# Block with expert retrieval on one core: scores picked by one-hot products, 896 output columns by a weight matrix built on chip

## The chip, the core and the metric

The kernel runs on one core of a Trainium2 chip. The core has TensorE (PE, matrix products), VectorE (DVE), ScalarE (ACT), GpSimd (POOL) and SyncE (SP), which run side by side, and 16 DMA engines that move data between memory (HBM) and the on-chip SBUF. PE writes its results into PSUM. The metric is device time in microseconds of one execution; lower is better.

## The reference

One decoder block on 256 tokens of 2,048 columns in float32: attention and retention with their projections, then a layer of retrieved experts, then a norm. The change touches the experts alone:

```python
expert_idx = ...                     # 8 heads x 16 chosen of 16,384 experts for each token
gates = jax.nn.softmax(best_s, axis=-1)
u = expert_down[ib]                  # chosen rows, 2,048 columns
act = jax.nn.gelu(jnp.einsum('td,thkd->thk', xb, u), approximate=False)
vv = expert_up[ib]
return jnp.einsum('thk,thkd->td', gb * act, vv)
```

Each token thus has 128 chosen experts. An expert's number is 128 i + j, with i and j from 0 to 127.

## The kernel before

Projections, attention, retention and the query's scores take the time up to about 892 us. Then `gemm1` runs: 32 tiles of 512 experts, in which TensorE multiplies all tokens with the first 1,408 columns of `expert_down`. Weights come as `raw` on SyncE's queue, ScalarE rounds them to `whi` (L107), VectorE subtracts to `wlo` (L108), and PE takes three products of the parts (L154 to L156); 384 of the 1,408 columns are multiplied as plain fp32 (L161), which the trace shows as two instructions for each product. Each finished tile is scaled on ScalarE (L467) and written to `a_dram`, a 256 x 16,384 table of scores (L468).

The remaining 640 columns are fetched for the chosen experts only. This goes on as background work beside `gemm1`: `later` queues steps with a cost, and `drain` lets so many through after each piece of a tile (`BG_RATE`, `BG_NATIVE`); top 16, candidates and ranks come first, then `indices` (L586), then 256 steps `dot`. Step n holds 128 tokens on partitions and one of their 128 choices: GpSimd fetches one row per token (L605, eight buffers), and VectorE multiplies by `hg` and sums along the columns in one instruction (L613).

After the last tile comes the tail. `score` (L640) picks one 4-byte number per token from `a_dram` on GpSimd, 256 times, 14 ahead; `fetch` (L583) brings 128 whole rows of `expert_up`, 1 MB, into one of eight buffers. Both are issued in one line on GpSimd. For eight choices at a time VectorE adds the score and the dot (L680), ScalarE takes Gelu (L681), VectorE multiplies by the gate (L682); then each fetched row is multiplied by its weight and added to `ys` in PSUM (L687, L689). `finish` adds the result to `h` (L659), takes squares (L661), multiplies by `fin` (L662), scales by the root and stores (L673). A scheduler that places each instruction on its engine sets the order; the program's text gives it priorities.

## Time and profile before

| what | us |
|---|---|
| median of three runs | 2114.41 (2112.65 to 2115.06) |
| the profiled execution | 2116.2 |
| its span in the trace | 2114.4 |
| PE busy | 1387.9 (66%) |
| DVE busy | 1556.2 (74%) |
| ACT busy | 614.7 (29%) |
| POOL busy | 918.4 (43%) |
| bytes moved by DMA | 630.24 MB, mean 298 GB/s |

The shares are means over stages with different limits, so a stage's own rows matter more: in the page's 40 slices PE shows nines up to two thirds of the span and zeros after, the DMA engines nines from about 970 us on, and the granted clock of PE falls from nine to five tenths where PE's work ends. A busy time counts an engine's instructions, not what it waits for; the granted clock says which of PE's two levels, 1.2 or 2.4 GHz, held.

### The profile page before, as it was taken

The page shows a single profiled execution, that of the slowest core. Times are in us where ns is not written, and L with a number is a line of the kernel's source. Part 1 is how long each engine was busy: PE and PEld are TensorE (multiplying, and loading weights), DVE is VectorE, ACT ScalarE, POOL GpSimd, SP SyncE. Part 2 cuts the span into 40 slices and gives each one's busy share as a digit, 9 for nine tenths or more (in the row PEclk, how much of TensorE's full clock was granted, in tenths as well). Part 3 has the DMA queues.
Part 4 walks back from the last instruction along what each step waited for, and adds up shares of the span by engine and source line. Part 5 has one row for each costly group of instructions (what it writes and reads, how often), then busy time and mean ns, then how long its engine had stood idle before and what let it go on. Part 6 is the DMA issues. An engine that isn't in the chain of part 4 may idle for free.

```text
span 2114.4 us, 18649 instructions
## 1 busy us (share of the span) xinstructions
PE 1387.9 (66%) x5864; PEld 1076.1 (51%) x5864; DVE 1556.2 (74%) x2037; ACT 614.7 (29%) x780; POOL 918.4 (43%) x802
## 2 busy tenths in 40 slices
...
GB/s 313 183 151 176 175 144 197 221 197 187 193 189 192 191 231 162 176 194 325 406 406 391 391 408 408 396 353 271 395 397 395 399 399 384 410 400 407 399 400 307
DMA packets 114516, 630.24 MB, mean 298 GB/s; under 512 B 21872, under 2 KB 22512, under 8 KB 54000
## 3 DMA queue, kind: packets, MB, share of 16 engines
...
## 4 chain that ended last, share of the span: by engine, by line
PE 47%; DMA 20%; issue 17%; POOL 8%; DVE 8%; POOLq 0%; ACT 0%; ACTq 0%; DVEq 0%; SPq 0%
PE acc L139 13%; PE acc L138 13%; PE acc L140 13%; DMA v<-in_down_g_dram,ix 11%; DMA v<-in_up_dram,ix 6%; DVE ys L689 4%; POOL v L583 4%; POOL wsel L640 3%; PE acc L161 2%; DMA wsel<-a_dram,ix 2%; DVE wlo L108 1%; PE acc L155 1%; PE acc L156 1%; PE acc L154 1%; POOL v L605 1%
## 5 line engine op out<-in xcount | busy, mean ns | idle before, releaser
L108 DVE TENSOR_TENSOR wlo<-raw,whi 128x1024 fp32r<-128x1024 f32 (+1 forms) x426 | 526.1, 1236 | 332.9 <-ACT whi L107 332.5
L107 ACT CAST whi<-raw 128x1024 fp32r<-128x1024 f32 (+1 forms) x426 | 443.8, 1048 | 667.7 <-PE acc L140 367.5
L689 DVE SCALAR_TENSOR_TENSOR ys<-v,wsel,ys 128x2048 f32<-128x2048 f32 x254 | 598.3, 2355 | 30.8 <-DMA v<-in_up_dram,ix 23.3
L605 POOL DMA_INDIRECT v<-in_down_g_dram,ix x256 | 347.5, 1357 | 353.0 <-ACT whi L107 273.0
L640 POOL DMA_INDIRECT wsel<-a_dram,ix x256 | 259.1, 1012 | 96.4 <-issue 93.0
L583 POOL DMA_INDIRECT v<-in_up_dram,ix x256 | 260.9, 1019 | 80.7 <-issue 58.7
L613 DVE SCALAR_TENSOR_TENSOR djunk<-v,rs_r,hg 128x640 bf16<-128x640 f32 x256 | 219.2, 880 | 99.6 <-DMA v<-in_down_g_dram,ix 99.0
L139 PE MATMUL acc<-wlo,xth 128*128 128x512 f32 x736 | 291.9, 397 | 0.0
L140 PE MATMUL acc<-whi,xtl 128*128 128x512 f32 x736 | 288.2, 392 | 0.0
L138 PE MATMUL acc<-whi,xth 128*128 128x512 f32 x736 | 266.7, 394 | 9.1 <-ACT whi L107 9.1
L155 PE MATMUL acc<-wlo,hth 128*128 128x512 f32 x512 | 203.8, 398 | 13.1 <-DVE wlo L108 12.9
L156 PE MATMUL acc<-whi,htl 128*128 128x512 f32 x512 | 200.1, 391 | 0.0
L154 PE MATMUL acc<-whi,hth 128*128 128x512 f32 x512 | 191.4, 411 | 2.2 <-ACT whi L107 2.2
L681 ACT ACTIVATE wsel<-wsel 128x8 f32<-128x8 f32 x32 | 6.6, 208 | 595.9 <-DVE wsel L680 533.7
L161 PE MATMUL acc<-raw,htf 128*128 128x512 f32 x384 | 169.9, 592 | 0.0
L138 PEld LDWEIGHTS acc<-whi,xth 128*128 128x128 f32 x736 | 138.7, 189 | 38.3 <-ACT whi L107 9.5
L139 PEld LDWEIGHTS acc<-wlo,xth 128*128 128x128 f32 x736 | 138.8, 189 | 29.7 <-DVE wlo L108 1.0
L140 PEld LDWEIGHTS acc<-whi,xtl 128*128 128x128 f32 x736 | 138.8, 189 | 28.1 <-issue 0.2
L433 POOL TENSOR_TENSOR sg<-sg 128x512 f32<-128x512 f32 x8 | 14.1, 1790 | 291.8 <-DVE sg L432 291.8
L155 PEld LDWEIGHTS acc<-wlo,hth 128*128 128x128 f32 x512 | 96.1, 188 | 42.9 <-DVE wlo L108 22.2
L154 PEld LDWEIGHTS acc<-whi,hth 128*128 128x128 f32 x512 | 96.1, 188 | 33.5 <-issue 12.2
L161 PEld LDWEIGHTS acc<-raw,htf 128*128 128x128 f32 x384 | 72.7, 189 | 79.1 <-issue 76.6
...
## 6 DMA issues: line engine op xcount, KB each, us to landing
raw<-in_w_in_dram SPq DMA_DIRECT2D x91, 1024.0 KB, 4.8
raw<-in_down_dram SPq DMA_DIRECT2D x64, 1024.0 KB, 8.9
...
raw<-in_w_rb_dram SPq DMA_DIRECT2D x16, 1024.0 KB, 4.8
raw<-in_w_out_dram SPq DMA_DIRECT2D x16, 1024.0 KB, 4.8
raw<-in_w_q_dram SPq DMA_DIRECT2D x16, 1024.0 KB, 4.8
...
raw<-in_w_ab_dram SPq DMA_DIRECT2D x8, 1024.0 KB, 4.9
```

The source lines that it names most:

```text
L107: nc.scalar.copy(hi[:, k:k + step], src)
L108: nc.vector.tensor_sub(lo[:, k:k + step], src, hi[:, k:k + step].bitcast(F32))
L138: nc.tensor.matmul(ps[b], lhsT=xh, rhs=wh, start=(c == 0), stop=False)
L139: nc.tensor.matmul(ps[b], lhsT=xh, rhs=wl, start=False, stop=False)
L140: nc.tensor.matmul(ps[b], lhsT=xl, rhs=wh, start=False, stop=(c == last))
L154: nc.tensor.matmul(ps[b], lhsT=xh, rhs=wh, start=(c == 0), stop=False)
L155: nc.tensor.matmul(ps[b], lhsT=xh, rhs=wl, start=False, stop=False)
L161: nc.tensor.matmul(ps[b], lhsT=xf[:, k, b * P:(b + 1) * P], rhs=nat[:, k], start=False, stop=(k == CN - 1))
L583: return nc.gpsimd.indirect_dma_start(v, None, up, IndirectOffsetOnAxis(ap=ix[:, 0, b, k:k + 1], axis=0), bounds_check=NE - 1)
L605: nc.gpsimd.indirect_dma_start(u[:, :GC], None, down_g, IndirectOffsetOnAxis(ap=ix[:, 0, b, k:k + 1], axis=0), bounds_check=NE - 1)
L640: return nc.gpsimd.indirect_dma_start(wsel[:, b, k:k + 1], None, a_flat, IndirectOffsetOnAxis(ap=ix[:, 1, b, k:k + 1], axis=0), bounds_che ...
L689: nc.vector.scalar_tensor_tensor(ys, v, w[:, kk:kk + 1], ys, op0=OP.mult, op1=OP.add)
```

## The change

Output columns 0 to 895 (`DC`) no longer come from fetched rows. For them a matrix W of weights is built in SBUF, one slice of 128 x 128 for each j: W[i, j, t] is the weight of expert 128 i + j for token t, zero where the expert wasn't chosen. Then the output is a dense product of W with all 16,384 rows of `expert_up` in those columns: 64 chunks of 917,504 B on SyncE's queue, two buffers `ud`, eight fp32 products of 448 columns each (L765). The other 1,152 columns (`VC`) are fetched as before, in five buffers (L617 to L620), and added on VectorE (L710, L712).

The build takes four tokens at a time, in two halves of 128 tokens (`W0`, `W1`):

- `extract` (L653): SyncE reads the four tokens' scores back from `a_dram` as `at`, i on partitions, j along (L657). For eight tokens at a time VectorE compares the chosen i with a row of numbers (L661), and ScalarE casts the result into `hot`, three buffers (L664). PE transposes each token's `hot` (L669), ScalarE copies it to `hotT` (L671), and PE multiplies with `at` (L674): row k then holds all 128 j of the choice k. VectorE compares with the chosen j, multiplies and sums (L678), which picks the score.
- `weigh` (L681): for eight tokens, add the dot (L684), Gelu on ScalarE (L685), times gate (L686).
- `place` (L688), up to three groups later: VectorE puts each weight into its column j (L695), PE multiplies `hot` with that (L699), ScalarE copies the result into W with a stride of 512 B (L700).

After each half PE transposes the weights (L749), VectorE copies them to `wsel` (L750), and from then on `add_row` may run for that half of the tokens. The text has 32 `add_row` steps in the second half of the build and 224 beside the dense stage. `indices` now transposes the chosen i, j and gates to choices on partitions (`selT`), and the dots are transposed after each 128. `DOT`, a dot's cost in the background queue, goes from 0.85 to 1.15; the dots have eight buffers of their own. Picks of scores on GpSimd, and the line they stood in, are gone. Buffers that `gemm1` used are closed ahead of the build, and the build's ahead of the dense stage, so that W and `ud` can take their place.

```diff
-DOT = 0.85
-VR = 8
-GRP = 8
-LEAD = 14
+DOT = 1.15
+UR = 8
+VR = 5
+DC = 896
+HC = DC // 2
+VC = D - DC
+JU = 2
...
-    a_flat = a_dram.rearrange("t (e o) -> (t e) o", o=1)
+    a_keys = a_dram.rearrange("t (i j) -> i t j", j=P)
...
-    ix = peer.tile([P, 2, NB, P], U32, name="ix")
-    vtiles = {}
-    vp = {}
-
-    def fetch(n):
-        v = vp["pool"].tile([P, D], F32, name="v", bufs=VR)
-        b, k = divmod(n, P)
-        vtiles[n] = v
-        return nc.gpsimd.indirect_dma_start(v, None, up, IndirectOffsetOnAxis(ap=ix[:, 0, b, k:k + 1], axis=0),
-                                            bounds_check=NE - 1)
+    ix = peer.tile([P, NB, P], U32, name="ix")
+    utiles, vtiles = {}, {}
+    pl = {}
 
     def indices():
+        ef = rp.tile([P, NB, P], F32, name="ef")
+        nc.vector.scalar_tensor_tensor(ef, sel[:, 0], 128.0, sel[:, 1], op0=OP.mult, op1=OP.add)
+        nc.vector.tensor_copy(ix, ef)
+        for k in range(3):
+            pt = ms.tile([P, T], F32, name="ms")
+            for b in range(NB):
+                nc.tensor.transpose(pt[:, b * P:(b + 1) * P], sel[:, k, b], ident)
+            nc.scalar.copy(selT[:, k], pt)
+        nc.vector.tensor_copy(selB, selT[:, 0])
+        nc.vector.tensor_copy(irow, iota[:, :, None].to_broadcast([P, P, 2]))
         rt.close()
         msk.close()
-        tmp2 = pool("tmp2")
-        ef = tmp2.tile([P, 2, NB, P], F32, name="ef")
-        nc.vector.scalar_tensor_tensor(ef[:, 0], sel[:, 0], 128.0, sel[:, 1], op0=OP.mult, op1=OP.add)
-        for b in range(NB):
-            nc.vector.tensor_scalar_add(ef[:, 1, b], ef[:, 0, b], rows[:, b:b + 1])
-        nc.vector.tensor_copy(ix, ef)
-        vp["pool"] = pool("v")
-        vp["ps"] = pool("ysum", space=PSUM)
-        for n in range(VR):
+        pl["v"] = pool("v")
+        pl["ys"] = pool("ysum", space=PSUM)
+        pl["ex_stack"], pl["pa_stack"] = ExitStack(), ExitStack()
+        pl["ex"] = pool("ex", stack=pl["ex_stack"])
+        pa = pl["pa"] = pool("pa", stack=pl["pa_stack"])
+        hg = pl["hg"] = pa.tile([P, NB, GC], F32, name="hg")
+        for b in range(NB):
+            nc.scalar.dma_start(hg[:, b], bass.AP(tensor=frow.tensor, offset=frow.offset + G0, ap=[[0, P], [1, GC]]))
+            nc.vector.tensor_mul(hg[:, b], h[:, b, G0:], hg[:, b])
+        for n in range(UR):
             fetch_u(n)
 
-    utiles = {}
-
     def fetch_u(n):
-        u = vp["pool"].tile([P, D], F32, name="v", bufs=VR)
+        u = pl["pa"].tile([P, GC], F32, name="u", bufs=UR)
         b, k = divmod(n, P)
-        nc.gpsimd.indirect_dma_start(u[:, :GC], None, down_g, IndirectOffsetOnAxis(ap=ix[:, 0, b, k:k + 1], axis=0),
+        nc.gpsimd.indirect_dma_start(u, None, down_g, IndirectOffsetOnAxis(ap=ix[:, b, k:k + 1], axis=0),
                                      bounds_check=NE - 1)
         utiles[n] = u
+
+    def fetch_v(n):
+        v = pl["v"].tile([P, VC], F32, name="v", bufs=VR)
+        b, k = divmod(n, P)
+        nc.gpsimd.indirect_dma_start(v, None, up_g, IndirectOffsetOnAxis(ap=ix[:, b, k:k + 1], axis=0),
+                                     bounds_check=NE - 1)
+        vtiles[n] = v
 
     def dot(n):
         u = utiles.pop(n)
         b, k = divmod(n, P)
-        junk = peer.tile([P, GC], BF16, name="djunk", bufs=2)
-        nc.vector.scalar_tensor_tensor(junk, u[:, :GC], rstd2[:, b:b + 1], hg[:, b], op0=OP.mult, op1=OP.mult,
+        junk = pl["pa"].tile([P, GC], BF16, name="djunk", bufs=2)
+        nc.vector.scalar_tensor_tensor(junk, u, rstd2[:, b:b + 1], pl["hg"][:, b], op0=OP.mult, op1=OP.mult,
                                        accum_out=sdot[:, b, k:k + 1])
-        if n + VR < NB * P:
-            fetch_u(n + VR)
-        else:
-            fetch(n + VR - NB * P)
-
-    later(4.0, indices)
+        if n + UR < NB * P:
+            fetch_u(n + UR)
+        if k == P - 1:
+            pt = acc.tile([P, 512], F32, name="acc")
+            nc.tensor.transpose(pt[:, :P], sdot[:, b], ident)
+            nc.scalar.copy(selT[:, 3, b * P:(b + 1) * P], pt[:, :P])
+
+    later(6.0, indices)
     for n in range(NB * P):
         later(DOT, dot, n)
 
...
     for t in range(NT):
         gemm1(t)
-    drain(1e9)
-
-    wsel = peer.tile([P, NB, P], F32, name="wsel")
+
     part3 = cst.tile([P, NB, 4], F32, name="part3")
     o_rows = out.rearrange("(b p) d -> p b d", p=P)
     total = NB * P
-
-    def score(n):
+    for st in reversed(right):
+        st.close()
+    wp = [ExitStack() for _ in range(NB)]
+    hots = {}
+    W = [pool("w0", stack=wp[0], side="right").tile([P, P, P], F32, name="W0")]
+
+    def extract(b, g):
+        ex = pl["ex"]
+        t0 = b * P + 4 * g
+        at = ex.tile([P, 4, P], F32, name="at", bufs=2)
+        nc.sync.dma_start(at, a_keys[:, t0:t0 + 4, :])
+        if g % 2 == 0:
+            hb = ex.tile([P, 4, P, 2], BF16, name="hb")
+            ids = selB[:, t0:t0 + 8].rearrange("p (a t) -> p a t", t=2)
+            nc.vector.tensor_tensor(hb, irow[:, None].to_broadcast([P, 4, P, 2]),
+                                    ids[:, :, None, :].to_broadcast([P, 4, P, 2]), op=OP.is_equal)
+            hot8 = ex.tile([P, 8, P], F32, name="hot", bufs=3)
+            nc.scalar.copy(hot8.rearrange("p (a t) i -> p a i t", t=2), hb)
+            hots[t0], hots[t0 + 4] = hot8[:, :4], hot8[:, 4:]
+        hot = hots[t0]
+        pt = acc.tile([P, 512], F32, name="acc")
+        for q in range(4):
+            nc.tensor.transpose(pt[:, q * P:(q + 1) * P], hot[:, q], ident)
+        hotT = ex.tile([P, 4, P], F32, name="hotT", bufs=2)
+        nc.scalar.copy(hotT, pt.rearrange("p (q k) -> p q k", q=4))
+        pr = acc.tile([P, 512], F32, name="acc")
+        for q in range(4):
+            nc.tensor.matmul(pr[:, q * P:(q + 1) * P], lhsT=hotT[:, q], rhs=at[:, q], start=True, stop=True)
+        for q in range(4):
+            t = t0 + q
+            junk = ex.tile([P, P], BF16, name="ejunk", bufs=2)
+            nc.vector.scalar_tensor_tensor(junk, iota, selT[:, 1, t:t + 1], pr[:, q * P:(q + 1) * P],
+                                           op0=OP.is_equal, op1=OP.mult, accum_out=wT[:, 0, t:t + 1])
+
+    def weigh(t0):
+        ts = slice(t0, t0 + 8)
+        w = wT[:, 1, ts]
+        nc.vector.tensor_add(w, wT[:, 0, ts], selT[:, 3, ts])
+        nc.scalar.activation(w, w, AF.Gelu)
+        nc.vector.tensor_mul(w, w, selT[:, 2, ts])
+
+    def place(b, g):
+        ex = pl["ex"]
+        t0 = b * P + 4 * g
+        hot = hots.pop(t0)
+        hw = ex.tile([P, 4, P], F32, name="hw", bufs=2)
+        for q in range(4):
+            t = t0 + q
+            nc.vector.tensor_scalar(hw[:, q], iota, selT[:, 1, t:t + 1], wT[:, 1, t:t + 1],
+                                    op0=OP.is_equal, op1=OP.mult)
+        pw = acc.tile([P, 512], F32, name="acc")
+        for q in range(4):
+            nc.tensor.matmul(pw[:, q * P:(q + 1) * P], lhsT=hot[:, q], rhs=hw[:, q], start=True, stop=True)
+        nc.scalar.copy(W[b][:, :, 4 * g:4 * g + 4].rearrange("p j t -> p t j"),
+                       pw.rearrange("p (q j) -> p q j", q=4))
+
+    ysum = {}
+
+    def add_row(n):
         b, k = divmod(n, P)
-        return nc.gpsimd.indirect_dma_start(wsel[:, b, k:k + 1], None, a_flat,
-                                            IndirectOffsetOnAxis(ap=ix[:, 1, b, k:k + 1], axis=0),
-                                            bounds_check=T * NE - 1)
-
-    line = {}
-
-    def in_line(fn, n):
-        if "last" not in line:
-            line["last"] = fn(n)
-            return
-        with tc.issue_after(line["last"].ins):
-            line["last"] = fn(n)
-
-    for n in range(LEAD):
-        in_line(score, n)
-
...
+        v = vtiles.pop(n)
+        if k == 0:
+            ysum[b] = pl["ys"].tile([P, VC], F32, name="ys")
+            nc.vector.tensor_scalar_mul(ysum[b], v, wsel[:, b, 0:1])
+        else:
+            nc.vector.scalar_tensor_tensor(ysum[b], v, wsel[:, b, k:k + 1], ysum[b], op0=OP.mult, op1=OP.add)
+        if n + VR < total:
+            fetch_v(n + VR)
+        if k == P - 1:
+            hs = h[:, b, DC:]
+            nc.vector.tensor_add(hs, ysum[b], hs)
+            square(b, slice(DC, D), 2)
+
+    def square(b, cols, i):
+        hs = h[:, b, cols]
+        n = cols.stop - cols.start
+        junk = pl["fin"].tile([P, VC], BF16, name="junk2", bufs=1)
+        nc.scalar.activation(junk[:, :n], hs, AF.Square, accum_out=part3[:, b, i:i + 1])
+        nc.vector.tensor_mul(hs, hs, pl["fbc"][:, cols])
+
+    for b in range(NB):
+        if b:
+            drain(1e9)
+            pl["pa_stack"].close()
+            W.append(pool("w1", stack=wp[1], side="right").tile([P, P, P], F32, name="W1"))
+        for g in range(P // 4):
+            extract(b, g)
+            if b == 0:
+                if g == 0:
+                    for n in range(VR):
+                        fetch_v(n)
+                drain(2.3)
+            if g % 2:
+                weigh(b * P + 4 * g - 4)
+                if g > 2:
+                    place(b, g - 3)
+                    place(b, g - 2)
+            if b:
+                add_row(g)
+        place(b, P // 4 - 2)
+        place(b, P // 4 - 1)
+        pt = acc.tile([P, 512], F32, name="acc")
+        nc.tensor.transpose(pt[:, :P], wT[:, 1, b * P:(b + 1) * P], ident)
+        nc.vector.tensor_copy(wsel[:, b], pt[:, :P])
+    pl["ex_stack"].close()
+
+    dn = pool("dn")
+    pl["fin"] = dn
+    fbc = pl["fbc"] = dn.tile([P, D], F32, name="fbc")
+    nc.scalar.dma_start(fbc, bass.AP(tensor=fin.tensor, offset=fin.offset, ap=[[0, P], [1, D]]))
+    pd = [[acc.tile([P, 512], F32, name="acc") for _ in range(2)] for _ in range(NB)]
+    for u in range(P // JU):
+        ud = dn.tile([P, JU, DC], F32, name="ud", bufs=2)
+        nc.sync.dma_start(ud, up[u])
+        for jj in range(JU):
+            j = u * JU + jj
+            for b in range(NB):
+                for c in range(2):
+                    nc.tensor.matmul(pd[b][c][:, :HC], lhsT=W[b][:, j, :], rhs=ud[:, jj, c * HC:(c + 1) * HC],
+                                     start=(j == 0), stop=(j == P - 1))
+
+    for n in range(P // 4, total):
+        add_row(n)
+    for b in range(NB):
+        for c in range(2):
+            cols = slice(c * HC, (c + 1) * HC)
+            nc.vector.tensor_add(h[:, b, cols], pd[b][c][:, :HC], h[:, b, cols])
+            square(b, cols, c)
...
-        "up": a["peer_expert_up"][0],
+        "up": a["peer_expert_up"][0][:, :DC].reshape(P, P // JU, JU, DC).transpose(1, 0, 2, 3),
+        "up_g": a["peer_expert_up"][0][:, DC:],
```

How the instructions stand in a row on their engines follows for two places; buffer numbers follow the tiles' names. First, ScalarE after the weights' last casts, before the change:

```order
L107 CAST whi_10791<-raw_10789 128x1024
L107 CAST whi_10795<-raw_10789 128x1024
L467 ACTIVATE a_10867<-acc_10809,rs2_r_5650 128x512
L467 ACTIVATE a_10867<-acc_10810,rs2_r_5650 128x512
L468 DMA a_dram_5665<-a_10867 128x2x512
L681 ACT_TABLE_LOAD
L681 ACTIVATE wsel_10871<-wsel_10871 128x8 x16
```

ScalarE in the middle of the build's first half, in the changed kernel:

```order
L671 COPY hotT_11103<-acc_11098 128x512
L671 COPY hotT_11125<-acc_11120 128x512
L700 COPY W0_10831<-acc_11148 128x4x128
L685 ACTIVATE wT_5684<-wT_5684 128x8
L700 COPY W0_10831<-acc_11159 128x4x128
L664 CAST hot_11242<-hb_11240 128x4x128x2
L671 COPY hotT_11176<-acc_11171 128x512
L671 COPY hotT_11198<-acc_11193 128x512
```

Where two operations for each eight choices stood, a round of six now repeats for each eight tokens: two `hotT` copies, a `W0` copy, Gelu, a `W0` copy, and the cast of the one-hot tile.

PE had no instruction after the last `gemm1` tile. In the same place of the build it now has these (`ident` marks the transposes):

```order
L669 MATMUL acc_11098<-ident_157,hot_11096 128x128 x4
L674 MATMUL acc_11105<-at_11092,hotT_11103 128x128 x4
L669 MATMUL acc_11120<-ident_157,hot_11096 128x128 x4
L674 MATMUL acc_11127<-at_11118,hotT_11125 128x128 x4
L699 MATMUL acc_11148<-hw_11143,hot_11012 128x128 x4
L699 MATMUL acc_11159<-hw_11154,hot_11012 128x128 x4
L669 MATMUL acc_11171<-ident_157,hot_11169 128x128 x4
```

The casts run two tiles ahead: between the copies from `hot_11096`, and the next from `hot_11169`, ScalarE casts `hot_11242`, which takes the buffer of `hot_11012`, the tile that the two place products read.

Second, VectorE in the tail before, where rows of 2,048 columns follow each other:

```order
L689 SCALAR_TENSOR_TENSOR ys_10915<-v_10963,wsel_10871,ys_10915 128x2048
L689 SCALAR_TENSOR_TENSOR ys_10915<-v_10971,wsel_10871,ys_10915 128x2048
L680 TENSOR_TENSOR wsel_10871<-wsel_10871,sdot_5675 128x8
L689 SCALAR_TENSOR_TENSOR ys_10915<-v_10979,wsel_10871,ys_10915 128x2048
L682 TENSOR_TENSOR wsel_10871<-wsel_10871,sel_5673 128x8
L689 SCALAR_TENSOR_TENSOR ys_10915<-v_10990,wsel_10871,ys_10915 128x2048
L689 SCALAR_TENSOR_TENSOR ys_10915<-v_10998,wsel_10871,ys_10915 128x2048
L689 SCALAR_TENSOR_TENSOR ys_10915<-v_11006,wsel_10871,ys_10915 128x2048
```

VectorE in the second half of the build, in the changed kernel:

```order
L678 SCALAR_TENSOR_TENSOR ejunk_12319,wT_5684<-iota_165,selT_5681,acc_12312 128x128
L712 SCALAR_TENSOR_TENSOR ys_12097<-v_12461,wsel_5685,ys_12097 128x1152
L678 SCALAR_TENSOR_TENSOR ejunk_12321,wT_5684<-iota_165,selT_5681,acc_12312 128x128
L678 SCALAR_TENSOR_TENSOR ejunk_12323,wT_5684<-iota_165,selT_5681,acc_12312 128x128
L686 TENSOR_TENSOR wT_5684<-wT_5684,selT_5681 128x8
L712 SCALAR_TENSOR_TENSOR ys_12097<-v_12492,wsel_5685,ys_12097 128x1152
L678 SCALAR_TENSOR_TENSOR ejunk_12344,wT_5684<-iota_165,selT_5681,acc_12339 128x128
L678 SCALAR_TENSOR_TENSOR ejunk_12346,wT_5684<-iota_165,selT_5681,acc_12339 128x128
L695 TENSOR_SCALAR hw_12355<-iota_165,selT_5681,wT_5684 128x128 x4
L695 TENSOR_SCALAR hw_12366<-iota_165,selT_5681,wT_5684 128x128 x4
L712 SCALAR_TENSOR_TENSOR ys_12097<-v_12544,wsel_5685,ys_12097 128x1152
```

Rows of 1,152 columns now stand between the picks, the weights and the columns that VectorE writes for PE. Of the 256 row operations 75 stand ahead of the second copy of `wsel`, and 181 behind it.

## Rows read from the trace of the kernel before

**Rows 1.** Windows by stage: us, each engine busy (instructions), granted clock, DMA share, GB/s

```profile
971.00:1412.00 441.00, 427.94 (x1570) 293.18 (x1569) 331.62 (x615) 140.95 (x155) 351.39 (x260) 1.00 1.01 399
1412.00:1436.00 24.00, 0.31 (x1) 0.00 (x0) 0.73 (x3) 2.35 (x4) 10.73 (x11) 0.57 0.32 130
1436.00:2102.00 666.00, 0.00 (x0) 0.00 (x0) 617.84 (x335) 13.04 (x44) 498.80 (x494) 0.50 0.99 392
```

**Rows 2.** Groups by form, VectorE: operation, count | busy us, mean ns | idle

```profile
L689 DVE SCALAR_TENSOR_TENSOR ys<-v,wsel,ys 128x2048 f32<-128x2048 f32 x254 | 598.3, 2355 | 30.8 <-DMA v<-in_up_dram,ix 23.3
...
L613 DVE SCALAR_TENSOR_TENSOR djunk<-v,rs_r,hg 128x640 bf16<-128x640 f32 x256 | 219.2, 880 | 99.6 <-DMA v<-in_down_g_dram,ix 99.0
...
L267 DVE TENSOR_TENSOR ra<-ra,rb 128x256 f32<-128x256 f32 x12 | 10.4, 870 | 2.7 <-POOL ra L265 2.4
...
L680 DVE TENSOR_TENSOR wsel<-wsel,sdot 128x8 f32<-128x8 f32 x32 | 5.4, 167 | 42.2 <-DMA wsel<-a_dram,ix 42.2
...
L268 DVE TENSOR_TENSOR ra<-ra,rb 128x256 f32<-128x256 f32 x12 | 5.0, 413 | 0.0
...
L563 DVE TENSOR_TENSOR oh<-oh 128x1024 bf16<-128x1024 bf16 x4 | 2.7, 678 | 0.0
...
L541 DVE SCALAR_TENSOR_TENSOR ext<-rf 128x128 f32<-128x128 f32 x2 | 0.5, 274 | 0.0
```

**Rows 3.** Timeline of VectorE at 961, 1388 and 1438 us: start, us, operation, count

```profile
961.18 0.48 DVE L593 TENSOR_SCALAR ef<-ef,rows 128x128 f32<-128x128 f32 x2
...
1387.58 0.87 DVE L613 SCALAR_TENSOR_TENSOR djunk<-v,rs_r,hg 128x640 bf16<-128x640 f32 x1
...
1388.39 0.87 DVE L613 SCALAR_TENSOR_TENSOR djunk<-v,rs_r,hg 128x640 bf16<-128x640 f32 x1
...
1438.00 9.53 DVE L689 SCALAR_TENSOR_TENSOR ys<-v,wsel,ys 128x2048 f32<-128x2048 f32 x4
```

**Rows 4.** Timeline of all engines from 881.98 us, a query score tile

```profile
881.98 1.05 PE L503 MATMUL ms<-sk,qt 128*128 128x128 f32 x8
...
882.87 0.60 PE L498 MATMUL ms<-ident,qs 128*128 128x128 f32 x4
...
883.07 0.59 ACT L505 COPY sc<-ms 128x512 f32<-128x512 f32 x1
```

**Rows 5.** Groups by form, ScalarE: the cast that splits weights

```profile
L107 ACT CAST whi<-raw 128x1024 fp32r<-128x1024 f32 x422 | 441.4, 1052 | 666.2 <-PE acc L140 367.5 <-DMA raw<-in_down_dram 197.7 <-PE acc L156 40.3
```

**Rows 6.** Timeline of TensorE: the last tile's fp32 products

```profile
1406.99 5.31 PE L161 MATMUL acc<-raw,htf 128*128 128x512 f32 x12
```

**Rows 7.** Windows of 8 us, TensorE alone: us, busy (instructions), clock, DMA share, GB/s

```profile
8.00:16.00 8.00, 5.47 (x22) 1.00 0.99 349
16.00:24.00 8.00, 7.81 (x27) 0.79 1.00 412
984.00:992.00 8.00, 4.96 (x16) 1.00 1.02 416
```

**Rows 8.** DMA queues, 1450 to 2000 us, then 1000 to 1380: packets, MB, share

```profile
q0 software_dynamic: 36608, 218.24, 100.3%
...
q0 software_dynamic: 18289, 74.94, 50.3%
q1 hardware_dynamic: 9729, 65.02, 42.6%
```

**Rows 9.** Timeline where scores turn to rows; then a load, KB each, us to landing

```profile
1413.06 0.37 ACTq L468 DMA_DIRECT2D a_dram<-a  x1
1422.22 1.02 POOL L640 DMA_INDIRECT wsel<-a_dram,ix  x1 [18.69 <-issue]
...
raw<-in_w_in_dram SPq DMA_DIRECT2D x91, 1024.0 KB, 4.8
```

**Rows 10.** Timeline of the end, VectorE and the last store

```profile
2102.41 2.48 DVE L659 TENSOR_TENSOR h<-ys,h 128x512 f32<-128x512 f32 x4
...
2109.53 0.94 SPq L673 DMA_DIRECT2D out_dram<-h  x2
```

68 lines of the change are left out of this document (21 added, 47 removed).

## The prediction

> **What bounds the kernel now.** Three views, in this order. First, windows by stage [rows 1]. Until 1412 us TensorE is the limit: it is busy for 427.94 of the last 441 us, at granted clock 1.00. A gap of 24 us follows. From 1436 to 2102 us PE is idle, and two resources share the limit: the DMA engines are 0.99 busy and VectorE works 617.84 of 666 us. Second, the groups of DVE [rows 2] and its timeline [rows 3]: a fetched row of 2,048 columns costs 2,355 ns, and four in a row take 9.53 us, so one costs 2.383 with the step to the next. Third, the DMA queues [rows 8]: fetched rows fill the engines for 100.3% of 550 us at 218.24 MB / 550 us = 396 GB/s. So bytes and VectorE must both shrink in this stage; TensorE is free there.
>
> **The bytes.** All 256 rows x 1,048,576 B are 268.4 MB. The change keeps 256 x 589,824 B = 151.0 MB and adds 58.7 MB of dense weights and a re-read of the scores (2 x 8.4 MB). The total falls, but only if the traffic can run. A row can be added only after its weight exists, and the weights now come from a chain on four engines in which the DMA engines have little to do.
>
> **Up to the build: 1426 us, no change.** Added to `gemm1`'s stage are three transposes of `sel`, two of `sdot`, two small loads and some copies; removed is one address operation. PE's own work sets the stage (97% busy), so I give it +-10 us and keep 1412. `DOT` 1.15 instead of 0.85 only spreads the dots; ten of them (0.81 us each, start to start, [rows 3]) now stand behind the last `wlo`, 8 us. Their cover is the last score write: issued at 1413.06, and the first score pick leaves at 1422.22 [rows 9]. If that cover went, 8 us would be added. The first read of scores waits for that write too; a 1 MB load landed in 4.8 us [rows 9], I take 4 for 256 KB: 1426.
>
> **First half of the build: 118 us.** Prices from rows: four 128x128 fp32 products .89 us to the next, 1.05 to the end; four transposes .60; a copy out of PSUM of 128x512 .59 [rows 4]; a cast of 128x1024 1.05 [rows 5]. (A product is two instructions in the trace.) PE works per 8 tokens as transposes, picks, transposes, picks, place, place, and ScalarE as two `hotT` copies, a `W0` copy, Gelu, a `W0` copy, the one-hot cast. The cast overwrites, of three buffers, the one that the second place has just read, so it can't start earlier; and the next `hotT` copy stands behind the cast on ScalarE. That closes a loop:
> place, place .89 + 1.05; W copy .05 + .59; cast 1.05; `hotT` .59 (its transposes ran meanwhile); .05 + picks .89; transposes .60 + .06; `hotT` .59 + .05; picks .89. Sum 7.35 us, times 16 = 118.
> VectorE needs less, per 4 tokens: four picks out of PSUM at .805 - 512 x 1.0476 ns = .27 (a dot has 512 columns more; the slope is (2355 - 880) / 1408 ns a column, [rows 2]), four weight columns at .24 [rows 3], half a one-hot compare .34 [rows 2], and .17 for two 8-column operations shared by 8 tokens: 2.55, or 82 us for the half. No row shows a pick from PSUM or the strided writes of the cast and the `W` copy. For the small operations I put the bounds at .17 (8 columns) and .28 (a 128-column operation, 274 ns) [rows 2]; for the two strided writes, at the contiguous price and twice it, which adds 1.64 x 16 = 26 us. I take the contiguous price, since the shape is that of [rows 4, 5].
>
> **Second half: 191 us.** The order shows that the scheduler drew rows forward: 75 of the 256 stand before the second copy of `wsel` on VectorE, 32 in the program text. One of 1,152 columns costs 2.383 - 896 x .0010476 = 1.445 us. So VectorE has 82 + 75 x 1.45 = 191 us in order against the chain's 118, and paces the half. Small operations at .17 or .28 move it by -22 to +6. DMA carries 44 MB in it, 232 GB/s, and isn't the limit.
>
> **Dense stage: 420 us.** 181 rows remain, 106.8 MB at 394 GB/s: 271 us; 58.7 MB of dense weights and 1 MB for the final norm at 402 GB/s: 149 us. The two rates are near the 396 of whole rows and the shares in `gemm1`'s stage, where 74.94 MB took 50.3% (392) and 65.02 MB took 42.6% (402) of 380 us [rows 8]; rows of 2,560 B there show that narrower rows lose nothing. PE needs 512 products x 2 x 448 columns. A 512-column one takes (5.31 - .59) / 11 = .429 us [rows 6], so 512 x 2 x .429 x 448/512 = 385. VectorE needs 181 x 1.45 = 262. DMA is last, PE next: were the bytes free, 385 would remain.
> The Trainium skill ("DMA: Bandwidth & Descriptors", section Where 436 GB/s comes from) says that memory gives one core about 358 GB/s; by it 166.5 MB would take an estimated 465 us, 45 more. The trace disagrees: 396 GB/s over 550 us [rows 8].
>
> **End: 15 us.** Before, the last row ended at 2102.41 and the last store was issued at 2109.53 [rows 10], the span ending at 2114.4: 12. Now two operations of 1,152 columns (1.4 each) and eight of 448 (.54, by four of 512 columns in 2.48, [rows 10]) stand there in place of eight of 512 (5.0): 15.
>
> **Sum.** 1426 + 118 + 191 + 420 + 15 = 2170 us of span. The profiled execution took 2116.2 with a span of 2114.4, and the median is 2114.41, so a span stands for the median. The rows' stage was 666 + 24 us; it becomes 309 us of build and 420 of dense work. So the 58.7 MB saved against whole rows are worth 148 us at 396 GB/s, but the first half moves almost no rows (118 lost) and the second moves 44 MB in 191 us instead of 112 (79 lost): some 50 us more than before, and the rest is in the start and the end.
>
> **The rivals.**
> (B) TensorE at 1.2 GHz. In one window PE was busy for 5.47 of 8 us; in the next the granted clock averaged .79 although PE was busy for 7.81. A window with 4.96 busy of 8, however, kept 1.00 [rows 7]. The build starts after a longer gap, in which .57 was granted [rows 1], and in its loop PE is busy 4.9 of 7.35 us. If it stays low, the PE terms (4.32 us) double: 11.67 x 16 = 187 in the first half, +69: 2239. For it: the low start. Against it: the row at 62% busy that kept full clock.
> (C) VectorE held up by GpSimd's row issue in the second half. Two additions of 256 columns took 870 beside GpSimd's work and 413 ns after it [rows 2]. GpSimd issues at 1.01 us each (498.80 / 494, [rows 1]): 75 rows are 76 of 191 us, 40%. 256 small operations x .46 x .4 = +47: 2217. Against it: the dots ran at 880 ns with rows being issued throughout. The Trainium skill ("SBUF — State Buffer", Who interferes with whom) says that some VectorE modes and GpSimd exclude each other at a shared port; the pair of rows agrees, the dots show no such hold.
> (D) The dense stream starves. It has two buffers: a chunk of 917,504 B must land while PE does one (6.0 us). At the share of 42.6%, 171 GB/s, it takes 5.4 us, and with some 2 us to start (4.8 us for 1 MB alone, against 2.6 at 400 GB/s) 7.6. Rows get the other 280 GB/s and last 381 us; 50 chunks pass meanwhile, and 14 more take 84: 465, or 2215. It decides when the stream's share falls under 230 GB/s.
> (E) The other side: the build runs at the busy time of its busiest engine. Then the first half is PE's 4.9 x 16 = 78 us, and at .17 for a small operation VectorE's second half is 60 + 109 = 169: 1426 + 78 + 169 + 420 + 15 = 2108. It decides if ScalarE's cast leaves the loop; both halves together must be under 249 us. Against it: the cast and the copies stand in one row on ScalarE, and three buffers tie the cast to the place.
> That the change doesn't do what it says (narrow rows costing like wide ones) has a row against it: 880 ns for 640 columns, 2,355 for 2,048.
>
> **How the numbers follow.** A difference under about 0.2%, 4 us, is what a measurement here can't tell from no change. The forecast, 2170, has a chance of .54; B .24; C .06; D .06; E .05; a sum that lands within 4 us of 2114 through the lower bounds only in part .05. So faster .05, same .05, slower .90. The forecast's own range is 2138 (small operations at .17, `gemm1` 10 early) to 2206 (strided writes at twice, `gemm1` 10 late). The range 2118 to 2242 takes in B, C and D and leaves out the two lower cases and the worst of B.
>
> **What would show it.** In the changed trace: the first scores read near 1422; 16 rounds of 7 to 8 us up to some 1545, with ScalarE's `hotT` copy waiting behind the cast and VectorE idle a third of the time; granted clock 1.00 in that half (near .5 means B); then VectorE over 90% busy to some 1735, small operations of 128 columns at .24 to .28 (longer only beside row issues means C); then DMA 0.98 or more for 420 us and PE over 85% busy, with PE waiting for `ud` seldom (often means D). It is wrong if the first half is far from 118 us, if the second isn't VectorE's, or if the last stage moves other than 400 GB/s.

## The result

The changed kernel takes 2258.74 us (median of four runs, 2238.3 to 2267.2), the kernel before 2114.73: a ratio of 1.0665, with a 95% interval of 1.059 to 1.074. The forecast was 2170, with a range of 2118 to 2242: it got right that the change is slower, but put the loss at 56 us where 144 were measured, outside the range. The profiled execution took 2254.59 us and spans 2252.8.

Windows by stage of the changed kernel (the columns are those of [rows 1]): first half of the build, second half, the dense stage while rows are still fetched, and what is left of it:

```profile
1419.00:1600.00 181.00, 128.49 (x633) 117.84 (x631) 86.53 (x432) 75.94 (x96) 0.00 (x0) 0.66 0.16 47
1600.00:1796.00 196.00, 105.89 (x637) 96.77 (x637) 184.68 (x510) 77.14 (x96) 79.89 (x79) 0.78 0.85 280
1797.00:2160.00 363.00, 319.99 (x815) 151.69 (x815) 250.81 (x177) 1.26 (x2) 173.32 (x172) 0.99 1.02 412
2160.00:2239.00 79.00, 78.80 (x211) 39.56 (x209) 7.11 (x7) 2.18 (x5) 0.00 (x0) 1.00 0.41 142
```

Against [rows 1] two stretches stand out. In the first half the granted clock is .66 and the DMA engines move 47 GB/s. In the last 79 us VectorE is done and TensorE works alone, with the DMA engines at .41. The second half is VectorE's, as forecast.

With marks in the trace (first score product on TensorE, first row added, first dense product, end of the last dense product or row) the sum of the forecast stands like this:

| stage | forecast | measured | difference |
|---|---|---|---|
| up to the build | 1426 | 1417 | -9 |
| first half | 118 | 184 | +66 |
| second half | 191 | 196 | +5 |
| dense stage | 420 | 443 | +23 |
| end | 15 | 13 | -2 |
| span | 2170 | 2253 | +83 |

(The build is counted here from 1416.62, the first score product on TensorE; in the table of runs below the half is counted from VectorE's first pick, 1418.7.)

One round of eight tokens in the first half, from the timeline (start us, us, engine, operation); lines between are left out:

```profile
1521.00 3.62 PE L699 MATMUL acc<-hw,hot 128*128 128x128 f32 x16
...
1522.95 1.03 ACT L700 COPY W<-acc 128x512 f32<-128x512 f32 x1 [3.87 <-PE acc L699]
...
1524.66 1.04 ACT L700 COPY W<-acc 128x512 f32<-128x512 f32 x1 [0.67 <-PE acc L699]
1525.50 1.98 ACT L664 CAST hot<-hb 128x1024 f32<-128x1024 bf16 x1
1527.26 0.64 ACT L671 COPY hotT<-acc 128x512 f32<-128x512 f32 x1
...
1527.95 1.40 PEld L674 LDWEIGHTS acc<-at,hotT 128*128 128x128 f32 x8 [2.90 <-ACT hotT L671]
...
1530.59 0.59 ACT L671 COPY hotT<-acc 128x512 f32<-128x512 f32 x1 [2.69 <-PE acc L669]
...
1531.22 1.78 PEld L674 LDWEIGHTS acc<-at,hotT 128*128 128x128 f32 x8 [1.13 <-ACT hotT L671]
...
1533.09 2.97 PE L699 MATMUL acc<-hw,hot 128*128 128x128 f32 x16
...
1535.05 1.05 ACT L700 COPY W<-acc 128x512 f32<-128x512 f32 x1 [3.87 <-PE acc L699]
```

From one `W` copy to the same one in the next round, 1522.95 to 1535.05, are 12.1 us; the next takes 11.8. The order of the forecast's loop is there: place products, `W` copies, cast, `hotT`, picks, `hotT`, picks, place. But the four picks take about 1.9 us to the next instruction (1531.22 to 1533.09) where .89 was put in, both places 3.62 and 2.97 where 1.94 was, and the `W` copy and the cast 1.03 and 1.98 where .59 and 1.05 were.

ScalarE's and TensorE's groups in that half, from 1430 to 1597 us (columns as in [rows 2]):

```profile
L700 ACT COPY W<-acc 128x512 f32<-128x512 f32 x30 | 30.7, 1033 | 57.9 <-PE acc L699 57.9
L664 ACT CAST hot<-hb 128x1024 f32<-128x1024 bf16 x14 | 27.7, 1976 | 0.0
L671 ACT COPY hotT<-acc 128x512 f32<-128x512 f32 x28 | 17.0, 607 | 40.6 <-PE acc L669 40.6
```

```profile
L674 PE MATMUL acc<-at,hotT 128*128 128x128 f32 x224 | 53.9, 416 | 49.5 <-ACT hotT L671 49.5
L699 PE MATMUL acc<-hw,hot 128*128 128x128 f32 x242 | 47.5, 378 | 0.1
```

In the dense stage, the DMA queues between 1800 and 2140 us (columns as in [rows 8]; the last line is of issues: count, KB each, median us to landing), and what PE waited for from 1797 to 2239 us (us, times, longest):

```profile
q0 software_dynamic: 23635, 96.83, 71.1%
q1 hardware_dynamic: 6768, 43.13, 30.6%
...
ud<-in_up_dram SPq DMA_DIRECT2D x48, 896.0 KB, 7.8
```

```profile
PE acc L765 <- DMA ud<-in_up_dram: 53.0, 42, 10.1
```

A chunk lands 7.8 us after its issue, and PE needs 6.0 for one (387 us for 64 where it never waits, in e4 below). With two buffers a chunk can be asked for only when the one two before it is done, so two periods are 7.8 + 6.0, or 6.9 us for one; 815 of the 1,024 instructions (two for each product) in 363 us are 7.1 for a chunk. The longest of the 42 waits, 10.1 us, ends at the first dense product and so lies before the stage; the other 41 cost PE 43 us of it. PE is also busy for 400 us in the stage instead of 387. The rows, whose queue takes 71.1%, are over 76 us before the dense work.

### The profile page after: what moved, and what is told of

Read it like the earlier page. It is cut to its first block, busy times and chain, and to the rows that moved or that the text cites. A ratio compares the mean times of both kernels' runs of the same rounds, so it can differ in the third digit from the quotient of the medians.

```text
span 2252.8 us, 24096 instructions
## 1 busy us (share of the span) xinstructions
PE 2027.0 (90%) x8178; PEld 1489.8 (66%) x8178; DVE 1470.1 (65%) x2835; ACT 764.3 (34%) x939; POOL 645.8 (29%) x546
## 3 DMA queue, kind: packets, MB, share of 16 engines
q8 instruction: 64, 1.05, 0.2%
## 4 chain that ended last, share of the span: by engine, by line
PE 65%; DMA 18%; issue 5%; ACT 4%; DVE 4%; POOL 3%; POOLq 0%; SPq 0%; ACTq 0%; DVEq 0%
PE acc L144 12%; PE acc L143 12%; PE acc L145 12%; PE acc L765 11%; DMA ud<-in_up_dram 9%; DMA u<-in_down_g_dram,ix 6%; PE acc L166 3%; PE acc L699 3%; PE acc L674 3%; POOL u L613 3%; PE acc L160 2%; PE acc L161 2%; PE acc L159 2%; ACT hot L664 2%; DVE ys L712 2%
## 5 line engine op out<-in xcount | busy, mean ns | idle before, releaser
L765 PE MATMUL acc<-ud,W 128*128 128x448 f32 x1024 | 399.7, 546 | 53.3 <-DMA ud<-in_up_dram 53.0
L613 POOL DMA_INDIRECT u<-in_down_g_dram,ix x256 | 335.9, 1312 | 373.7 <-DVE hb L661 276.9
L712 DVE SCALAR_TENSOR_TENSOR ys<-v,wsel,ys 128x1152 f32<-128x1152 f32 x254 | 360.8, 1421 | 117.3 <-DMA v<-in_up_g_dram,ix 114.2
L620 POOL DMA_INDIRECT v<-in_up_g_dram,ix x256 | 259.0, 1012 | 493.9 <-DVE ys L710 196.4
L765 PEld LDWEIGHTS acc<-ud,W 128*128 128x128 f32 x1024 | 191.7, 191 | 260.8 <-issue 183.8
L628 DVE SCALAR_TENSOR_TENSOR djunk<-u,rs_r,hg 128x640 bf16<-128x640 f32 x256 | 216.4, 881 | 64.5 <-DMA u<-in_down_g_dram,ix 64.1
L674 PE MATMUL acc<-at,hotT 128*128 128x128 f32 x512 | 101.3, 359 | 90.5 <-ACT hotT L671 78.9
L674 PEld LDWEIGHTS acc<-at,hotT 128*128 128x128 f32 x512 | 86.6, 255 | 107.5 <-ACT hotT L671 95.4
L724 ACT ACTIVATE junk<-h 128x448 bf16<-128x448 f32 (+1 forms) x6 | 4.6, 772 | 449.0 <-DVE h L717 376.3
L699 PE MATMUL acc<-hw,hot 128*128 128x128 f32 x512 | 102.4, 374 | 49.1 <-DVE hw L695 49.1
```

What stands on the lines that cost most here:

```text
L613: nc.gpsimd.indirect_dma_start(u, None, down_g, IndirectOffsetOnAxis(ap=ix[:, b, k:k + 1], axis=0), bounds_check=NE - 1)
L620: nc.gpsimd.indirect_dma_start(v, None, up_g, IndirectOffsetOnAxis(ap=ix[:, b, k:k + 1], axis=0), bounds_check=NE - 1)
L674: nc.tensor.matmul(pr[:, q * P:(q + 1) * P], lhsT=hotT[:, q], rhs=at[:, q], start=True, stop=True)
L712: nc.vector.scalar_tensor_tensor(ysum[b], v, wsel[:, b, k:k + 1], ysum[b], op0=OP.mult, op1=OP.add)
L765: nc.tensor.matmul(pd[b][c][:, :HC], lhsT=W[b][:, j, :], rhs=ud[:, jj, c * HC:(c + 1) * HC], start=(j == 0), stop=(j == P - 1))
```

## The experiments

Twelve more kernels ran, on different chips: the kernel before took 2123.7 us beside e1 to e4, 2154.0 and 2154.7 beside e5 to e9 (one chip), 2115.9 beside e10 and 2116.7 beside e11 and e12. Runs on different chips are therefore compared by their stages. The ratio to the kernel before holds for one chip only: e5 and e12 have nearly the same ratio, 1.0127 and 1.0132, though e12's stages are 31 us shorter in all. The marks of the trace give (us):

| run | first pick at | first half | second half | dense stage | median time |
|---|---|---|---|---|---|
| changed kernel | 1418.7 | 181.5 | 196.4 | 442.9 | 2258.7 |
| e1 | 1431.0 | 134.4 | 198.8 | 447.7 | 2227.1 |
| e2 | 1424.7 | 161.5 | 199.6 | 452.9 | 2253.8 |
| e3 | 1417.0 | 181.8 | 196.4 | 465.7 | 2279.5 |
| e4 | 1426.7 | 174.7 | 196.3 | 413.5 | 2229.6 |
| e5 | 1431.3 | 123.1 | 196.4 | 413.1 | 2181.7 |
| e6 | 1424.0 | 123.6 | 219.7 | 404.1 | 2189.1 |
| e7 | 1425.6 | 123.1 | 194.9 | 414.3 | 2176.3 |
| e8 | 1428.0 | 162.8 | 197.1 | 387.6 | 2194.5 |
| e9 | 1434.6 | 160.7 | 191.3 | 388.1 | 2188.9 |
| e10 | 1430.2 | 123.0 | 189.2 | 391.6 | 2153.0 |
| e11 | 1420.1 | 181.2 | 197.6 | 421.1 | 2240.6 |
| e12 | 1433.8 | 112.3 | 190.0 | 399.6 | 2147.6 |

(The stages are those of the profiled execution, which took 2254.6 us for the changed kernel and 2156.1 for e12; e1 to e4, e7 and e11 ran once. In e8 to e10 the first half ends with the first row whose weight comes from `wsel`.) The start moves by up to 18 us, since the last write of scores is issued between 1409.3 (e3) and 1426.8 (e9); why it comes later in some runs stays open. Code that an experiment left alone varies too: the first half took 181.8 and 181.2 us in e3 and e11 at a granted clock of .66, but 174.7 in e4 at .70, and the dense stage 442.9 to 452.9 in the changed kernel, e1 and e2.

**e1: does the clock set the first half?**

```diff
+    def warm(last, n):
+        for _ in range(n):
+            with tc.issue_after(last.ins):
+                last = nc.tensor.matmul(pl["wm"][:, :T], lhsT=selB[:, :P], rhs=irow.rearrange("p k t -> p (k t)"),
+                                        start=True, stop=True)
...
+        if b == 0 and g % 2:
+            warm(last, 3)           # behind the second transposes
...
+        if b == 0 and g % 2:
+            warm(last, 12)          # behind the second place
```

> Edit: in the first half of the build PE gets products whose result nobody reads, 12 of 256 bf16 columns after each second place and 3 after each second group of transposes, in the gaps of its loop. Theory (TensorE at 1.2 GHz doubles its terms of the loop, the strided writes of ScalarE add about 0.9): granted clock rises from the 0.6 to 0.8 of the changed kernel to at least 0.95, a round of 8 tokens falls from 11.6 to about 8.3 us, the first half from 184 to some 135 us, the time from 2255 to some 2205. Rival (the loop is set by ScalarE's copies and by the waits between engines, and the clock is only a sign of the gaps): the clock rises but a round stays at 11 us or more, the time within 15 us of 2255. If the fillers don't raise the clock, they lengthen the round and neither is told apart.

Windows of e1, first and second half, and TensorE's groups from 1435 to 1560 us (L683 picks, L708 place, L657 the unread products):

```profile
1431.00:1565.00 134.00, 104.21 (x863) 93.43 (x862) 86.50 (x431) 74.87 (x95) 0.00 (x0) 0.99 0.22 64
1565.00:1764.00 199.00, 110.78 (x650) 101.95 (x648) 186.26 (x513) 77.71 (x96) 80.20 (x80) 0.76 0.83 276
```

```profile
L683 PE MATMUL acc<-at,hotT 128*128 128x128 f32 x240 | 34.8, 288 | 29.8 <-ACT hotT L680 29.8
L708 PE MATMUL acc<-hw,hot 128*128 128x128 f32 x229 | 28.0, 275 | 0.0
L657 PE MATMUL wm<-irow,selB 128*128 128x256 bf16 x213 | 28.0, 273 | 0.0
```

More work made the half 47 us shorter. The granted clock is .99 there, a pick takes 288 ns instead of 416, a place 275 instead of 378, and a round 8.67 us (from one `W` copy at 1499.97 to the same one of the next round at 1508.64), close to the 8.3 that was expected. In the second half, which has no such products, the clock stays at .76 (.78 in the changed kernel) and the half at 198.8 us. The rival, a round of 11 us or more at the higher clock, falls. The time fell by 28 instead of 50 us against the changed kernel's profiled execution, since this run's build began 12 us later and its last two stages took 7 more.

**e2: what does the stride of the cast cost?**

```diff
-            nc.vector.tensor_tensor(hb, irow[:, None]..., ids[:, :, None, :]..., op=OP.is_equal)
-            nc.scalar.copy(hot8.rearrange("p (a t) i -> p a i t", t=2), hb)
+            nc.vector.tensor_tensor(hb, irow[:, None]..., selB[:, t0:t0 + 8, None]..., op=OP.is_equal)
+            nc.scalar.copy(hot8, hb)
```

> Edit: the one-hot compare and the cast write in contiguous order (token, then number) instead of pairs of tokens. Theory (the write with a stride makes the cast 1.98 instead of 1.05 us): the cast takes 1.05 us, a round about 0.85 less (11.6 to 10.7), the first half 184 to 170. The compare may lose its 0.69 us and take 1.2, which costs the second half, where VectorE sets the pace, 16 x 0.5 = 8 us; the time about 2249. Rival (the cast costs 1.98 because of its source in bf16, not of the stride): the cast stays at 1.9 or more and the first half at 184.

ScalarE's groups from 1430 to 1585 us of e2 (L699 is the `W` copy, L663 the cast):

```profile
L699 ACT COPY W<-acc 128x512 f32<-128x512 f32 x30 | 30.0, 1029 | 52.6 <-PE acc L698 52.6
...
L663 ACT CAST hot<-hb 128x1024 f32<-128x1024 bf16 x15 | 15.7, 1049 | 0.0
```

The cast takes 1.05 us from a bf16 source too, so its 1.98 was the stride. The first half is 20 us shorter, more than the 14 expected; its granted clock was .71 instead of .66, so the rest isn't put down to the cast. The compare takes 1.23 instead of .69, and the second half 3 us more. The time, 2253.8 where 2249 was expected, is that of the changed kernel: the later start, the second half and the dense stage took back what the first half had gained.

**e3 and e4: the stream of dense chunks.**

```diff
-VR = 5
+VR = 4                                                   # e3
-        ud = dn.tile([P, JU, DC], F32, name="ud", bufs=2)
+        ud = dn.tile([P, JU, DC], F32, name="ud", bufs=3)
```

```diff
-JU = 2
+JU = 1                                                   # e4
-        ud = dn.tile([P, JU, DC], F32, name="ud", bufs=2)
+        ud = dn.tile([P, JU, DC], F32, name="ud", bufs=4)
```

> Edit: three buffers for the dense chunks instead of two, and four for fetched rows instead of five (for room). Theory (a chunk lands 7.7 us after its issue while PE needs 5.9 for one, so with two buffers the period is (7.7 + 5.9) / 2 = 6.8 us until the rows are over, and the dense work that is left runs alone for 70 us): period near 6.0 us, PE over 95% busy in the stage, the stage 443 to some 405 us, the time some 2215. Rival (the stage is set by the bytes and by which queue gets them; what the stream gains the rows lose): PE's share and the stage unchanged within 10 us, the time 2245 to 2265.

> Edit: dense chunks of half the size (3,584 B for each partition instead of 7,168) with four buffers, the same bytes in flight; nothing else. Theory (a buffer comes free too late): a smaller chunk is freed and asked for earlier, the stage falls from 443 to about 410 us, the time to some 2220. Rival (the queues share by packets, and half as long packets halve the stream's share): PE's share falls under 0.85 while rows run, the stage grows by 10 us or more, the time 2265 or more.

Windows of e4, until the last dense product and after it, and its queues from 1800 to 2140 us:

```profile
1798.00:2184.00 386.00, 386.00 (x1023) 195.34 (x1023) 231.72 (x164) 1.26 (x2) 160.82 (x160) 1.00 1.00 399
2184.00:2211.00 27.00, 0.60 (x2) 0.00 (x0) 24.30 (x20) 0.00 (x0) 12.03 (x12) 0.56 0.75 262
```

```profile
q0 software_dynamic: 21281, 87.17, 63.9%
q1 hardware_dynamic: 16139, 51.41, 38.3%
...
ud<-in_up_dram SPq DMA_DIRECT2D x113, 448.0 KB, 6.7
```

With smaller chunks PE is busy without a break for 386 us, and the stage takes 413.5. The DMA engines are full as long as the dense products last, but not in the 27 us behind them, when the last 16 rows are added. VectorE's timeline shows what kept those rows:

```profile
2182.38 0.62 DVE L773 TENSOR_TENSOR h<-acc,h 128x448 f32<-128x448 f32 x1 [15.39 <-PE acc L765]
```

The first addition of the dense result (L773) stands ahead of the last rows, and VectorE waits 15 us before TensorE's last products. So neither the bytes nor PE alone set this stage; e12 below, with these additions behind the rows, takes 399.6. The stream's packets are half as long (51.41 MB / 16,139 against 43.13 MB / 6,768), yet its share grew from 30.6 to 38.3%, so the rival falls: what counted was how soon a chunk is asked for.

e3 also brought PE to its 387 us, but took longer in all. Its VectorE's timeline shows why:

```profile
2123.50 2.88 DVE L712 SCALAR_TENSOR_TENSOR ys<-v,wsel,ys 128x1152 f32<-128x1152 f32 x2 [2.15 <-DMA v<-in_up_g_dram,ix]
2180.43 0.62 DVE L773 TENSOR_TENSOR h<-acc,h 128x448 f32<-128x448 f32 x1 [54.05 <-PE acc L765]
2180.97 1.41 DVE L712 SCALAR_TENSOR_TENSOR ys<-v,wsel,ys 128x1152 f32<-128x1152 f32 x1
```

Here the scheduler had set the same addition ahead of 43 rows; VectorE stood 54 us before TensorE's last products, with rows waiting. **e11** is e3 with these additions behind the last row:

```diff
+            with tc.issue_after(pl["row"].ins):          # the last fetched row
+                nc.vector.tensor_add(h[:, b, cols], pd[b][c][:, :HC], h[:, b, cols])
```

> The run with three dense buffers and four row buffers again, and VectorE's additions of the dense result now stand behind its last fetched row. There, 43 rows stood behind the first of these additions and waited 54 us for TensorE's last product. Theory (with three buffers the stream no longer starves, and only this order undid the gain): the dense products again take 387 us with PE over 98% busy, the rows end about when the bytes allow, 166.5 MB at 402 to 412 GB/s, 404 to 414 us after the stage begins; the time about 2222 where the two-buffer form takes 2255. Rival (four row buffers are too few beside a stream that is never late): the rows end 430 us or more after the stage begins, the time 2240 or more.

The dense products take 387 us and the stage 421: between the 414 and the 430 that were to tell the two apart. The time, 2240.6 where 2222 was expected, even lies on the rival's side; 5 us of that are the additions, which now stand behind the last row (18.8 us from there to the end instead of 13.3). The order cost 45 us in e3, that much is shown; whether four row buffers cost the other 7 is left open.

**e5: do the gains add up?** e1, e4, and e2 in the first half alone. The unread products stand in the first half only, not in both as the expectation says.

> The three edits that helped, together: the unread products in both halves of the build, the contiguous compare and cast in the first half alone (the second keeps the changed kernel's form), dense chunks of half the size with four buffers. Theory (three separate causes, each with its own place: clock and stride in the first half, the stream's buffers in the last stage): they add up. First half 134 - 13 = 121 us, second half unchanged at 196 to 200 since VectorE sets it, last stage 412, the time 2255 - 47 - 13 - 27 = about 2168. Rival (the gains cover each other: with the clock held, the cast no longer matters, or the earlier rows meet the same limit of bytes): less than half of the sum, 2205 or more.

First half 123.1 (121 expected), second 196.4, dense stage 413.1 (412): the gains lie in separate stages and add, if the cast is counted at its own 13 us and not at the 20 that e2's half lost. The time is 2181.7 where 2168 was expected, since the build began 12.6 us later than in the changed kernel. The ratio is 1.0127 (1.0097 to 1.0156).

**e6: is the second half VectorE's?**

```diff
-            nc.vector.tensor_scalar(hw[:, q], iota, ...)
+            (nc.gpsimd if b else nc.vector).tensor_scalar(hw[:, q], iota, ...)
```

> As the three edits together, and in the second half GpSimd instead of VectorE writes the weight columns for PE (128 operations of 128 columns). Theory (VectorE's own work sets the second half): VectorE loses 128 x 0.27 = 34 us; the order draws 84 rows instead of 75 into the half, 9 x 1.42 = 13 back, which the last stage then saves; the second half 197 to about 176, the last stage 412 to 399, the time some 34 us under the run beside it, about 2134. Rival (the chain of PE, ScalarE and now GpSimd sets the second half, for GpSimd's operations and row issues stand in one row): the second half stays at 190 or more, VectorE idles 20 us more in it, the time within 15 us of the run beside it.

GpSimd's groups and two waits in the second half of e6:

```profile
L712 POOL TENSOR_SCALAR hw<-iota,selT,wT 128x128 f32<-128x128 f32 x128 | 100.8, 795 | 1.4
L623 POOL DMA_INDIRECT v<-in_up_g_dram,ix x85 | 88.8, 1045 | 161.8 <-DVE ys L729 136.5 <-issue 14.1 <-DVE ejunk L695 5.7
```

```profile
PE acc L716 <- POOL hw L712: 66.6, 63, 4.9
...
DVE ys L731 <- DMA v<-in_up_g_dram,ix: 42.0, 49, 2.0
```

One such operation takes GpSimd 795 ns, where VectorE needs .27 us, and with 85 row issues GpSimd is busy for 190 of 220 us. PE now waits for it 66.6 us, and VectorE for rows 42. The half grew by 23 us against e5, as the rival had it; a new engine took the place of the old one, so this run doesn't tell what the half would be with less of VectorE's work.

**e7: the cast taken out of the loop.** Added to e5, in the first half alone:

```diff
-                nc.vector.tensor_tensor(hv, irow1[:, None]..., selB[:, t0:t0 + 8, None]..., op=OP.is_equal)
-                nc.scalar.copy(hot8, hv)
+                nc.vector.tensor_tensor(hot8, irow1[:, None]..., selB[:, t0:t0 + 8, None]..., op=OP.is_equal)
```

> As the three edits together, and in the first half VectorE writes the one-hot tile in float32 itself (1.23 us for eight tokens, as with bf16), so that ScalarE's cast, 1.05 us of the loop, is gone there. Theory (the loop of the first half is place, two W copies, cast, hotT, picks, transposes, hotT, picks): a round falls from 7.7 to about 6.75 us, the first half from 123 to some 108, the time 15 us under that of the three edits. Rival (VectorE, busy for 90 of 122 us, or PE with its unread products sets the round once the cast is gone): the first half stays at 118 or more.

The half stays at 123.1. Timeline from the place products on (`wm` are the unread products):

```profile
1505.00 1.47 PE L659 MATMUL wm<-irow,selB 128*128 128x256 bf16 x12
...
1506.31 0.60 PE L682 MATMUL acc<-ident,hot 128*128 128x128 f32 x4
...
1507.00 0.59 ACT L686 COPY hotT<-acc 128x512 f32<-128x512 f32 x1 [0.71 <-PE acc L682]
1507.64 0.97 PEld L689 LDWEIGHTS acc<-at,hotT 128*128 128x128 f32 x8 [0.97 <-ACT hotT L686]
```

Twelve unread products now stand between place and the next transposes, and `hotT` waits .71 us for these; the cover that the cast had been is gone. The remedy of e1 had become part of the loop, one of the two causes that the rival named. A round is 7.74 us here and 6.88 in e12, which has 4 such products and contiguous `W` copies; the two weren't tried apart.

**e8, e9, e10: early rows.** In e8 GpSimd picks the scores of 24 choices as the kernel before does, and their rows are added in the first half:

```diff
+                if b == 0 and 4 <= g < 4 + ER:          # ER = 24
+                    if g % 8 == 4:
+                        weigh_early(g - 4)              # add the dot, Gelu, times gate, for eight
...
+                    add_row(g - 4)
```

e9 adds row-major `W`:

```diff
-        nc.scalar.copy(W[b][:, :, 4 * g:4 * g + 4].rearrange("p j t -> p t j"), ...)
+        nc.scalar.copy(W[b][:, 4 * g:4 * g + 4, :], ...)
...
-                    nc.tensor.matmul(..., lhsT=W[b][:, j, :], ...)
+                    nc.tensor.matmul(..., lhsT=W[b][:, :, j], ...)
```

> The same, and 24 rows of the first 128 tokens are added in the first half already: their scores are picked by GpSimd from memory as in the kernel before (1.31 us each), their weights made on the side. Theory (VectorE has some 30 us to spare in the first half; the last stage, 412 us, is bound by bytes down to PE's own 387): the first half grows by 0 to 10 us, the second stays (76 rows in the order), the last stage has 157 rows instead of 181 left and falls to 387, the time about 25 to 35 us under the run beside it without early rows, at or just under the kernel before. Rival (in the first half the rows take VectorE from the loop, 24 x 1.44 = 35 us, and all 24 picks stand ahead of the rows on GpSimd): the first half grows by 25 us or more and nothing is won.

> The same with the early rows, and W is kept as token by j, so that ScalarE's copies into it are contiguous, and TensorE loads its weights from W with a stride of 512 B instead. Theory (the write with a stride costs 1.04 instead of 0.59 us, a weight load with a stride costs nothing): the copies take 0.59, a round 0.4 to 0.5 less, the first half 7 us less, the last stage the same 387, the time 5 to 8 us under the run beside it. Rival (the load pays for the stride): a weight load of the dense product takes over 0.25 instead of 0.19 us, or the last stage grows by 10 us or more.

Two waits in the first half of e8 (`remote` is a release that the trace does not name), and the weight loads and copies of `W` in e9 (shortest, median, longest ns):

```profile
DVE ejunk L704 <- remote: 20.0, 2, 17.4
...
ACT W L728 <- remote: 16.3, 1, 16.3
```

```profile
L812 PEld LDWEIGHTS acc<-ud,W x1024: 291/295/333, 1786.6 to 2173.8; 128*128 128x128 f32 x171
...
L728 ACT COPY W<-acc x64: 586/586/638, 1464.5 to 1777.9; 128x512 f32<-128x512 f32 x64
```

The last stage fell to 388 us in both, as expected with fewer rows left. But the first half of e8 grew by 40, the rival's case. In one stretch, from 1440 to 1458 us, VectorE and ScalarE stand for 17 and 16 us; it ends just behind the last of the 24 score fetches, which GpSimd issues one by one from 1424 to 1455. What they waited for the trace doesn't say; the first addition for the early weights had run before it, at 1439.75. From 1462 to 1528 the rows then keep VectorE busy for 65 of 66 us. In e9 the copies take 586 ns, and a weight load with a stride 295 instead of 190, as the rival had it; the dense stage doesn't feel it (388.1 against 387.6), since a load runs beside the product before. The first half lost 2 us by the shorter copies, not the 7 expected. The ratios are 1.0187 (1.0169 to 1.0206) and 1.0154 (1.0136 to 1.0173).

e10 is e9 with fewer and later early rows, and fewer unread products:

```diff
-            warm(last, 12)
+            warm(last, 4)
...
+            if b == 0 and 12 <= g < 12 + ER:            # ER = 16
+                if g == 12:
+                    weigh_early()                       # behind the picks of that group
+                add_row(g - 12)
```

> The row-major W and the one-hot tile written by VectorE as in the run before, 4 instead of 12 unread products after each second place, and 16 instead of 24 early rows, whose weights VectorE takes up only in the twelfth group of four tokens, when their picks have long landed. Theory (the early rows cost 38 us in the first half because VectorE stood before their picks, and the dense stage is PE's 387 us as soon as at most 165 rows are left for it): the first half 110 to 120 us, the second 190, the last stage 387 to 392, the time 2140 to 2150 where the kernel before takes 2154, a ratio of 0.993 to 0.998. Rival (rows in the first half lengthen its loop wherever they stand, since every operation of VectorE in it is waited for by PE or ScalarE): the first half 135 us or more, the ratio 1.004 or more.

In e10, with 16 rows from the twelfth group on, the first half takes 123.0, the second 189.2, the dense stage 391.6. The stages are close to the expectation, the first half 3 us above it, and the stretch in which VectorE stood is gone; yet the same half without early rows takes 112.3 in e12, so the 16 rows still lengthen it by 11. The ratio is 1.0171 (1.0147 to 1.0196), on the rival's side: the expected ratio had been reckoned against the 2154 of another chip. Which part of the kernel before is longer on that chip no trace here shows.

**e12: everything that helped.** e7 with row-major `W`, 4 unread products instead of 12, and the additions of e11 behind the last row; no early rows.

> The one-hot tile by VectorE, W row by row, 4 unread products after each second place, dense chunks of half the size with four buffers, no early rows, and the additions of the dense result behind the last fetched row. Theory (each of these takes its own piece: a round of the first half 6.7 to 7.0 us, so 108 to 112 for the half, the second half 190, the last stage 412 less the 8 us that rows waited behind the dense additions, the end 15): start 1430, 1540, 1730, 2135, so about 2150 on a chip where the kernel before takes 2115 and a ratio near 1.016; nothing of it beats the kernel before, since first half and second half together still move only 48 MB in 300 us. Rival (with the first half at 110 us and the bytes of the last stage at 404 GB/s the sum reaches the kernel before): a ratio of 1.004 or less.

Windows of e12 by stage:

```profile
1434.00:1546.00 112.00, 93.79 (x744) 83.86 (x743) 90.95 (x432) 43.89 (x84) 0.00 (x0) 0.97 0.26 76
1546.00:1736.00 190.00, 104.66 (x641) 95.89 (x638) 184.41 (x511) 63.97 (x95) 79.79 (x79) 0.79 0.86 287
1736.00:2136.00 400.00, 387.38 (x1024) 302.68 (x1024) 254.37 (x180) 1.26 (x2) 173.30 (x172) 0.98 1.02 404
```

A round takes 6.88 us, the first half 112.3, the second 190.0, the dense stage 399.6, where 112, 190 and 404 were expected at most; the end takes 18.7 where 15 was put in. The ratio is 1.0132 (1.0112 to 1.0153), where 1.016 was expected. With every mended piece in it the build still moves only 76 GB/s for 112 us and 287 for 190. No version here beats the kernel before.

## Why the prediction was wrong

- **The bytes are not the saving:** right. The build moves 47 and 280 GB/s in its halves, and that gave the gain back; in e12 it does so even with everything else mended.
- **Up to the build, 1426:** 9 us too late for this execution. The first read of scores was put behind a write that landed in 9 us [rows 9]. There the DMA engines were full until 1417 us and .95 busy until 1419; here they are .28 busy from 1410 to 1412, and the write, issued at 1410.85, had landed when the read was issued at 1413.64. Over all runs the start varies by 18 us, and 1426 lies in that spread.
- **First half, 118 us:** the step that failed, 66 of the 83 us. Two terms of the loop were mis-sized. The first is TensorE's clock. The terms of PE were taken at full clock because a window at 62% busy had kept it [rows 7], and rival B got a chance of .24. But TensorE idles for 6.5 us before the build, .50 is granted from 1414 to 1430 us, and in its loop the gaps come again in every round; the granted clock averaged .66. e1 shows the clock to be the cause of 47 us. The kept clock of [rows 7] was one wait of 3.09 us between windows of 8 us with PE busy for 7.95 and 8.00; it said nothing about a loop that begins at 1.2 GHz and waits in every round. The Trainium skill ("TensorE: Matmul & The Clock Gate", section A second HAM failure mode: psum-queue depth-cycling) tells of a kernel whose short idle times between groups of products let the clock go up and down; the trace agrees, with .66 granted on the mean of the half, and in the round shown eight weight loads take 1.40 and then 1.78 us (.97 at full clock, in e7). Rival B had put the half at 187 with TensorE at 1.2 GHz throughout; that 184 lies near it is in part luck, since the clock was between the levels and the strided writes made up the rest.
- The second term is the two writes with a stride. Their price was known to be open, the bounds were one and two times the contiguous price, and the lower was taken because the shapes agreed. The shape was the wrong thing to go by: the order of the elements decides, 1,976 and 1,033 ns here against 1,049 (e2) and 586 (e9). For the cast the runs show what it cost the half, 11 us with the clock held (e1 to e5); for the `W` copy alone only the 2 us of e9 are measured. With the clock held and the cast contiguous (e5) the half takes 123.1, near the 118. The Trainium skill ("SBUF — State Buffer", section Door 1: The DMA port swizzle) says that an access pays when it crosses to a new 16-byte line of SBUF; these writes do so at every element, and the trace agrees.
- **Second half, 191 us:** right, 196. VectorE is busy for 184.68 of it, and the three groups that were priced from neighbours came out nearly as put in:

```profile
L712 DVE SCALAR_TENSOR_TENSOR ys<-v,wsel,ys 128x1152 f32<-128x1152 f32 x78 | 110.5, 1416 | 0.1
L678 DVE SCALAR_TENSOR_TENSOR ejunk<-iota,selT,acc 128x128 bf16<-128x128 f32 x128 | 39.4, 339 | 0.6 <-PE acc L674 0.6
L695 DVE TENSOR_SCALAR hw<-iota,selT,wT 128x128 f32<-128x128 f32 x128 | 34.5, 340 | 0.0
```

The row costs 1,416 ns where 1.445 us with its step was put in; a pick lasts 339 ns, but the first two start at 1418.70 and 1418.97, .27 apart as put in. A weight column costs .27 us (34.5 for 128) where .24 was put in. Rival C didn't come: beside GpSimd's row issues a pick and a column take 339 and 340 ns, and 343 and 341 in the first half, where GpSimd issues none. Not all of the half was VectorE's: with contiguous `W` copies it takes 190.0 (e12) instead of 194.9 (e7). That VectorE's work sets the rest is read from its busy time; no run took work off it without slowing something else.
- **Dense stage, 420 us:** the bytes run faster than forecast, 412 GB/s while rows flow, and there are fewer of them, 161 MB (364 GB/s over 442.9 us) instead of 166.5. The 358 GB/s of the Trainium skill ("DMA: Bandwidth & Descriptors", section Where 436 GB/s comes from) are not seen here either. But the limit was a mean over the stage. Rival D, put at .06, is what happened, for a cause that it named: two buffers and a stream slower than PE. It put the rows at 381 us with a chunk every 7.6, and 84 us for the chunks left over; the rows took 367 with a chunk every 7.1, and 76 us were left: 443 and not 465. e4 takes 29 us away by smaller chunks with the same bytes in flight, and e12, with the additions behind the last row, 43.
- **End, 15 us:** 13. The terms given add up to 14, and the operations of 1,152 columns came long before the end, at 2163.64 and 2166.38.
- **The range:** B and D were counted as cases that exclude each other, each added to 2170 alone. They have different places and nothing in common; both came, B in part, and so did nearly the upper bound of the strided writes. A range of 2118 to 2242 could hold only one of them.
